# Up projection of a ConvFFN: two products of the next pair put between the third and fourth of the current one, and one weight sum moved from POOL to DVE

## The chip, the cores and the metric

The kernel runs on one core of a Trainium2 chip, in float32. The metric is the device time of one execution in microseconds; the time of a kernel is the median of its runs. TensorE is PE in the rows (its weight loads are PEld), VectorE is DVE, ScalarE is ACT, GpSimd is POOL and SyncE, which issues most DMAs, is SP.

## The reference, cut to what matters

One decoder block with three sublayers, each followed by a LayerNorm of `ALPHA * x + sublayer`: token mixing by two groups of heads, a cross-attention to a memory, and a gated ConvFFN. The change lies in the first half of the ConvFFN, on x of 1024 x 1024, `w_up` of 1024 x 5632 and a causal convolution of width 3:

```python
D_MODEL, SEQ, D_FF, CONV_WIDTH = 1024, 1024, 2816, 3

def _conv_ffn(x, w_up, conv_w, conv_b, w_down):
    u = jnp.einsum('bsd,df->bsf', x, w_up)
    ch = u.shape[-1]
    u = lax.conv_general_dilated(u, conv_w.reshape(CONV_WIDTH, 1, ch).astype(u.dtype),
                                 window_strides=(1,), padding=[(CONV_WIDTH - 1, 0)],
                                 dimension_numbers=('NWC', 'WIO', 'NWC'),
                                 feature_group_count=ch) + conv_b
    a, g = jnp.split(u, 2, axis=-1)
    return jnp.einsum('bsf,fd->bsd', jax.nn.silu(g) * a, w_down)
```

## The kernel before, in words

The stages follow one another: input projection, the two mixers, their output projection and LayerNorm, the cross-attention, its output projection and LayerNorm, then the up projection (with convolution and gate) and the down projection. Nothing is scheduled by hand between engines: the program is written in one order, a scheduler lays out each engine's queue from it, and an engine works its queue strictly in that order, waiting where an operand is not there. In the profiled execution the up projection lies at about 929 to 1383 us of the span.

**Pairs and products.** The up projection goes over NF = 22 pairs f of 128 columns of the a half and 128 columns of the g half of `w_up`. One pair is a 2x2 block product in the Strassen-Winograd form: seven block products in place of eight, on sums and differences of the blocks. On the weight side these are A11, A12, A22 (blocks as they are) and S3, S1, S2, S4 (sums and differences; S2 is made from S1, S4 from S2). On the side of x they are B11, B21, B22 and T3, T1, T2, T4, made once for all pairs. Each operand is split into a high part (a cast to fp32r) and a low part (the rest), and a product is 12 matmuls of 128x512 with 12 weight loads: for each of four k, high by high, high by low, low by high. The product's line is L1080.

**The order of a pair.** `begin(f)` does A11 with B11 into a bank of tag `S`, copies it to `ya` (L1089, ACT), does A12 with B21 into a bank of tag `pj` and adds it to `ya` (L1091, DVE). `end(f)` does S3 with T3 into a first `t` bank (copied to `yg` by L1109, ACT), S1 with T1 into a second `t` bank (added to `yg` by L1111, DVE), S2 with T2 on top of A11's bank (copied to `u` by L1114, ACT, and added to `yg` by L1115, DVE), A22 with T4 on top of S3's bank (L1117, DVE), and S4 with B22 on top of S1's bank (L1121, DVE). So A22 may not start before L1109 has read its bank, nor S4 before L1111 has. There are two `pj`, three `t` and three `S` banks. Between A22 and S4 the g half goes through its convolution (`conv`: L1099 on ACT, L1100 and L1101 on DVE) and silu (L1119, ACT); after S4 the a half goes through the convolution, L1123 multiplies the two, and L1125 writes `hid`. Up to pair 10 (HC = 11), L1128 also takes a difference for the down projection and L1129 writes it to `sum`. Before, the pairs stand as `begin(0)`, `begin(1)`, `end(0)`, `begin(2)`, `end(1)`, `begin(3)` and so on (LEAD = 2).

**The weights.** `Weights` makes them up to six (WAHEAD) ahead of their use, in the order of the products. For each product `load` takes the source, casts it to the high part on ACT (L1046) and subtracts on POOL to get the low part (L1047). A source is raw columns of `w_up` (a DMA, L1013, into one of three `raw` buffers) or a sum at L1024: S3 and S1 on POOL, S2 and S4 on DVE. The sums S1 and S2 share one slot (`sw`), S3 and S4 another.

**Slots.** Nearly every tile (`wop`, `sw`, `ya`, `yg`, `z`, `s3`, the operands) is one of 47 slots of equal size. They go round first in, first out, so a new tile waits for the last reader or writer of an old one in the same slot, also for a DMA that writes an old `z` or `s3` to memory.

**The operands of x.** B11 and B21 are made during the LayerNorm before. T3, T1, T2, T4 and B22 are made by `turn` at their first use, in pair 0: transposes on TensorE (L991), a copy on ACT (L993), a subtraction on DVE (L994).

The down projection follows in L1244, with operands made by L183 (ACT) and L185 (POOL or DVE). Its first weights go into slots that come free near the end of the up projection.

## Time and profile before

| | |
|---|---|
| runs | 1615.91, 1626.25, 1627.2 us; median 1626.25 us |
| profiled execution | 1620.13 us, of which its span is 1618.4 us |
| mean granted clock of TensorE | 0.988 of full speed |
| PE | 1552.2 us busy, 96% of the span |
| PEld | 1307.9 us, 81% |
| DVE | 1104.0 us, 68% |
| ACT | 739.8 us, 46% |
| POOL | 642.8 us, 40% |
| up projection, 929 to 1383 us: PE, DVE, POOL, ACT | 437.24, 330.54, 316.94 and 212.27 of 454.00 us |

The profile is one execution of its own, recorded by the hardware, so its time differs a little from the median; the execution's time is its span and 1.7 us around it. Busy shares are averages over stages with different limits. The matmuls of PE overlap one another, so PE counts as busy also where a short wait lies between two of them; the weight loads (PEld) show the waits more sharply.

### The profile page before, as it was taken

To read this page: it belongs to the slowest core of one execution; us is meant where nothing else is said; L and a number is where in the kernel's file an instruction comes from. 1 tells how busy PE (TensorE), PEld (TensorE's weight loads), DVE (VectorE), ACT (ScalarE), POOL (GpSimd) and SP (SyncE) were. 2 spreads that over 40 slices of the span, in tenths; PEclk is the share of its full clock that TensorE was granted. 3 is DMA by queue.
4 is the path that set the end of the run, shared out by engine and by line. 5 is a ranking of instruction groups with operands and counts; after the bars stand their busy time and mean duration, and the time that the engine had idled before them with its cause. 6 is when DMAs were issued, how large, how long until landed. Compare 5 with 4: busy or idle time off the path is not lost.

```text
span 1618.4 us, 21414 instructions
## 1 busy us (share of the span) xinstructions
PE 1552.2 (96%) x7949; PEld 1307.9 (81%) x7949; DVE 1104.0 (68%) x1734; ACT 739.8 (46%) x1317; POOL 642.8 (40%) x496
## 2 busy tenths in 40 slices
PE   8999999999998989999999999999989999999996
PEld 6788888888887988888978878777768888788884
DVE  4856967466667756642556567777777667987896
ACT  4725564255566751133542144444445455445531
POOL 5303222134435741111102657877778775000043
PEclk9999999999999999999999999999999999999998
DMA  5301112132141592311382222322223224875753
GB/s 183 79 1 27 53 53 59 47 92 67 52 118 46 170 267 89 120 40 52 104 263 92 78 66 69 100 86 87 89 94 95 79 79 134 282 245 184 235 189 104
DMA packets 166041, 176.67 MB, mean 109 GB/s; under 512 B 7761, under 2 KB 122521, under 8 KB 165937
## 3 DMA queue, kind: packets, MB, share of 16 engines
q1 hardware_dynamic: 162448, 163.61, 32.5%
q10 hardware_dynamic: 3168, 11.54, 1.9%
q8 instruction: 62, 1.02, 0.3%
q14 instruction: 43, 0.34, 0.1%
q0 software_dynamic: 320, 0.16, 0.1%
HBM read 132.77 MB, written 38.31 MB: 106 GB/s over the span
## 4 chain that ended last, share of the span: by engine, by line
PE 61%; DVE 15%; DMA 8%; POOL 6%; ACT 4%; issue 4%; SPq 1%; POOLq 0%; DVEq 0%; ACTq 0%
PE ps_pj L174 22%; PE ps_S L174 17%; PE ps_t L1080 7%; PE ps_t L174 5%; PE ps_S L1080 3%; POOL wop L1047 3%; DVE dop L185 2%; DMA raw<-hid 2%; POOL sw L1024 2%; DMA raw<-sumS 2%; DVE sw L1024 2%; PE ps_pj L1080 2%; PE ps_S L1244 1%; DVE z L1101 1%; DVE z L1100 1%
## 5 line engine op out<-in xcount | busy, mean ns | idle before, releaser
L174 PE MATMUL ps_pj<-xT,wh 128*128 128x512 f32 x976 | 313.6, 397 | 0.9 <-DVE KL L593 0.9
L174 PEld LDWEIGHTS ps_pj<-xT,wh 128*128 128x128 f32 x976 | 180.5, 189 | 35.2 <-DVE KL L593 1.4
L185 POOL TENSOR_TENSOR wl<-raw,wh 128x1024 fp32r<-128x1024 f32 x48 | 118.0, 2457 | 219.7 <-ACT wh L183 206.2
L174 PE MATMUL ps_pj<-xT,wl 128*128 128x512 f32 x488 | 193.0, 395 | 0.0
L1080 PE MATMUL ps_t<-T,wop 128*128 128x512 f32 x792 | 190.2, 391 | 1.5 <-ACT yg L1109 0.9
L1080 PEld LDWEIGHTS ps_t<-T,wop 128*128 128x128 f32 x792 | 148.1, 188 | 33.5 <-ACT yg L1109 1.3
L784 POOL TENSOR_SCALAR mv<-mv 128x1 f32<-128x1 f32 x24 | 27.0, 1123 | 342.0 <-DVE mv L783 342.0
L1047 POOL TENSOR_TENSOR wop<-raw,wop 128x512 fp32r<-128x512 f32 x66 | 119.7, 1826 | 94.4 <-ACT wop L1046 94.4
L1047 POOL TENSOR_TENSOR wop<-sw,wop 128x512 fp32r<-128x512 f32 x88 | 135.6, 1562 | 28.9 <-ACT wop L1046 28.9
L1244 PE MATMUL ps_S<-dop,dop 128*128 128x512 f32 x396 | 102.8, 405 | 8.8 <-DVE dop L185 6.0
L1046 ACT CAST wop<-sw 128x512 fp32r<-128x512 f32 x88 | 54.5, 621 | 124.1 <-POOL sw L1024 106.5
L174 PEld LDWEIGHTS ps_pj<-xT,wl 128*128 128x128 f32 x488 | 91.9, 188 | 17.7
L174 PE MATMUL ps_S<-wh,mh 128*128 128x512 f32 x256 | 100.1, 391 | 0.7 <-ACT mh L183 0.7
L174 PE MATMUL ps_S<-wh,ml 128*128 128x512 f32 x256 | 100.2, 392 | 0.0
L1244 PEld LDWEIGHTS ps_S<-dop,dop 128*128 128x128 f32 x396 | 76.8, 196 | 28.7 <-DVE dop L185 8.1
L174 PE MATMUL ps_S<-wl,mh 128*128 128x512 f32 x256 | 99.9, 390 | 0.0
L183 ACT CAST wh<-raw 128x1024 fp32r<-128x1024 f32 x64 | 67.2, 1049 | 61.2 <-issue 23.6
L1244 PE MATMUL ps_t<-dop,dop 128*128 128x512 f32 (+1 forms) x351 | 87.1, 378 | 1.7 <-DVE y L1295 1.7
L183 ACT CAST dop<-raw 128x512 fp32r<-128x512 f32 x77 | 47.7, 622 | 85.7 <-DVE raw L1209 44.9
L1080 PE MATMUL ps_t<-B,wop 128*128 128x512 f32 x264 | 68.9, 410 | 13.6 <-DVE yg L1111 13.6
L1244 PEld LDWEIGHTS ps_t<-dop,dop 128*128 128x128 f32 x351 | 63.5, 189 | 14.1 <-DVE y L1295 1.9
L1080 PEld LDWEIGHTS ps_t<-B,wop 128*128 128x128 f32 x264 | 50.8, 196 | 28.3 <-DVE yg L1111 17.8
(301 smaller groups left out, 3584.5 us busy)
## 6 DMA issues: line engine op xcount, KB each, us to landing
raw<-in_ffn_w_up_dram SPq DMA_DIRECT2D x44, 512.0 KB, 3.9
raw<-hid SPq DMA_DIRECT2D x66, 256.0 KB, 3.4
raw<-in_w_in_dram SPq DMA_DIRECT2D x24, 512.0 KB, 4.0
hid<-z SPq DMA_DIRECT2D x22, 512.0 KB, 2.6
wr<-in_ffn_w_down_dram SPq DMA_DIRECT2D x44, 256.0 KB, 4.7
raw<-sumS SPq DMA_DIRECT2D x44, 256.0 KB, 3.8
raw<-in_xa_wkv_dram SPq DMA_DIRECT2D x16, 512.0 KB, 4.4
x_dram<-y ACTq DMA_DIRECT2D x16, 512.0 KB, 2.6
```

The costliest lines, as they stand in the source:

```text
L174: nc.tensor.matmul(o, l, r, start=start, stop=stop)
L183: nc.scalar.copy(h, src)
L185: eng.tensor_tensor(l, src, h.bitcast(F32), ALU.subtract)
L784: nc.gpsimd.tensor_scalar(mv[:, 2:3], mv[:, 1:2], LN_EPS, None, ALU.add)
L1024: eng.tensor_tensor(sums[pair][:, i], x0, x1, op)
L1046: nc.scalar.copy(w[:, 0], src)
L1047: nc.gpsimd.tensor_tensor(w[:, 1], src, w[:, 0].bitcast(F32), ALU.subtract)
L1080: nc.tensor.matmul(ps, w[:, part, ws], r, start=first and k == 0 and i == 0, stop=k == 3 and i == 2, skip_group_check=not first)
L1100: nc.vector.scalar_tensor_tensor(z[:, 1:], y[:, :S - 1], c1, z[:, 1:], ALU.mult, ALU.add)
L1101: nc.vector.scalar_tensor_tensor(z[:, 2:], y[:, :S - 2], c0, z[:, 2:], ALU.mult, ALU.add)
L1244: nc.tensor.matmul(groups[g][t][:, lo:hi], x[:, xp, ss], w[:, wp, lo:hi], start=first and i == 0 and n == 0, stop=i == HC - 1 and n == 2, ...
```

## The change

Two things are changed. The first is the order of the products, and with it the order in which the weights are made: `begin(f + 1)` is called inside `end(f)`, after L1115 and ahead of A22, where `begin(f + 2)` stood behind `end(f)`. Before, the products of a pair and what followed were S3, S1, S2, A22, S4, then A11 and A12 of f + 2; now they are S3, S1, S2, then A11 and A12 of f + 1, then A22 and S4. `begin(0)` and `begin(1)` still stand ahead of the loop, so `end(0)` has no `begin` in it. B11 and B21 give back their slots after `end(20)`; before, it was after `begin(21)`. The second is that the sum S1 is made on DVE in place of POOL. `take` fills up its store of weights from the first `begin` on, by a list `begun` in place of `live`.

```diff
--- before.py
+++ after.py
@@ -1031,7 +1031,7 @@
             if name == "S3":
                 return add("S3", self.rawt(f, 0)[:, 0], self.rawt(f, 1)[:, 0], ALU.subtract, nc.gpsimd)
             if name == "S1":
-                return add("S1", self.rawt(f, 1)[:, 0], self.rawt(f, 1)[:, 1], ALU.add, nc.gpsimd)
+                return add("S1", self.rawt(f, 1)[:, 0], self.rawt(f, 1)[:, 1], ALU.add, nc.vector)
             if name == "S2":
                 return add("S2", sums["S1S2"][:, 0], self.rawt(f, 0)[:, 0], ALU.subtract, nc.vector)
             assert name == "S4"
@@ -1052,20 +1052,22 @@
             self.ready.append(((f, name), w))
 
         def take(self, f, name):
-            while self.todo and len(self.ready) < 1 + (self.ahead if live or name == "S3" else 0):
+            while self.todo and len(self.ready) < 1 + (self.ahead if begun else 0):
                 self.load()
             key, w = self.ready.pop(0)
             assert key == (f, name)
             return w
 
     LEAD = 2
-    first, later = [("A11", "B11"), ("A12", "B21")], [("S3", "T3"), ("S1", "T1"), ("S2", "T2"), ("A22", "T4"),
-                                                      ("S4", "B22")]
-    order = [(f, a) for f in range(LEAD) for a, _ in first]
+
+    first = ["A11", "A12"]
+    order = [(f, a) for f in range(LEAD) for a in first]
     for f in range(NF):
-        order += [(f, a) for a, _ in later]
-        if f + LEAD < NF:
-            order += [(f + LEAD, a) for a, _ in first]
+        order += [(f, a) for a in ("S3", "S1", "S2")]
+        if LEAD <= f + 1 < NF:
+            order += [(f + 1, a) for a in first]
+        order += [(f, a) for a in ("A22", "S4")]
+    begun = []
     weights = Weights(order, WAHEAD)
     live = {}
 
@@ -1090,6 +1092,7 @@
         product(f, "A12", "B21", pe, True)
         nc.vector.tensor_tensor(ya[:, hs(0)], ya[:, hs(0)], pe, ALU.add)
         live[f] = ya, yg, pa
+        begun.append(f)
 
     def conv(f, j, y):
 
@@ -1113,6 +1116,8 @@
         u = small.tile([P, 512], F32, tag="vT", name="u", bufs=1)
         nc.scalar.copy(u, pa)
         nc.vector.tensor_tensor(yg[:, hs(1)], yg[:, hs(1)], u, ALU.add)
+        if LEAD <= f + 1 < NF:
+            begin(f + 1)
         product(f, "A22", "T4", pc, False)
         nc.vector.tensor_tensor(yg[:, hs(0)], u, pc, ALU.add)
         zg = conv(f, 1, yg)
@@ -1154,11 +1159,9 @@
         begin(f)
     for f in range(NF):
         end(f)
-        if f + LEAD < NF:
-            begin(f + LEAD)
-            if f + LEAD == NF - 1:
-                for name in ("B11", "B21"):
-                    put(*[t for p in ops.pop(name) for t in p])
+        if f == NF - 2:
+            for name in ("B11", "B21"):
+                put(*[t for p in ops.pop(name) for t in p])
     for o in ops.values():
         put(*[t for p in o for t in p])
 
```

The changed file is a few lines longer. These lines of before read in it: L1080 as L1082, L1089 as L1091, L1091 as L1093, L1099 to L1101 as L1102 to L1104, L1109 as L1112, L1111 as L1114, L1114 as L1117, L1115 as L1118, L1117 as L1122, L1119 as L1124, L1121 as L1126, L1123 as L1128, L1125 as L1130, L1128 as L1133 and L1244 as L1247. L991, L1013, L1024, L1046 and L1047 keep their numbers. Note that L1091, L1117 and L1128 are other operations in the two files.

Three places show what it does to the queues. The first is DVE's queue around the convolutions of pair 4, whose g half is `z_9476` and whose a half is `z_9497`; `sw` are weight sums of a pair further on. Before:

```order
L1100 SCALAR_TENSOR_TENSOR z_9476<-yg_9219,cw,z_9476 128x1023
L1121 TENSOR_TENSOR ya_9218<-u,ps_t 128x512
L1101 SCALAR_TENSOR_TENSOR z_9476<-yg_9219,cw,z_9476 128x1022
L1100 SCALAR_TENSOR_TENSOR z_9497<-ya_9218,cw,z_9497 128x1023
L1101 SCALAR_TENSOR_TENSOR z_9497<-ya_9218,cw,z_9497 128x1022
L1091 TENSOR_TENSOR ya_9506<-ya_9506,ps_pj 128x512
L1123 TENSOR_TENSOR z_9497<-z_9497,z_9476 128x1024
L1128 TENSOR_TENSOR s_480_9503<-z_9497 128x512
L1111 TENSOR_TENSOR yg_9363<-yg_9363,ps_t 128x512
L1024 TENSOR_TENSOR sw_9583<-sw_9583,raw 128x512
L1024 TENSOR_TENSOR sw_9565<-raw,sw_9583 128x512
L1115 TENSOR_TENSOR yg_9363<-yg_9363,u 128x512
```

And in the changed kernel, from the same operation on `z_9476`:

```order
L1103 SCALAR_TENSOR_TENSOR z_9476<-yg_9278,cw,z_9476 128x1023
L1126 TENSOR_TENSOR ya_9277<-u,ps_t 128x512
L1104 SCALAR_TENSOR_TENSOR z_9476<-yg_9278,cw,z_9476 128x1022
L1024 TENSOR_TENSOR sw_9545<-raw 128x512
L1103 SCALAR_TENSOR_TENSOR z_9497<-ya_9277,cw,z_9497 128x1023
L1024 TENSOR_TENSOR sw_9545<-sw_9545,raw 128x512
L1104 SCALAR_TENSOR_TENSOR z_9497<-ya_9277,cw,z_9497 128x1022
L1114 TENSOR_TENSOR yg_9422<-yg_9422,ps_t 128x512
L1024 TENSOR_TENSOR sw_9527<-raw,sw_9545 128x512
L1128 TENSOR_TENSOR z_9497<-z_9497,z_9476 128x1024
L1118 TENSOR_TENSOR yg_9422<-yg_9422,u 128x512
L1133 TENSOR_TENSOR s_480_9503<-z_9497 128x512
```

Before, the two sums that DVE makes (S2, S4) stood together behind the whole pair and behind L1111 of the next one. Now there are three, S1, S2 and S4 in this order; S1 and S2 stand between the convolution's steps, and S4 behind L1114 (L1111 of before), which itself moved ahead of the multiplication.

The second place is ACT's queue between the silu of pair 4 and the first convolution step of pair 5 (`z_9620`), with the semaphores that each operation waits for. Those that begin with DMAHW count finished transfers. Before:

```order
L1119 ACTIVATE z_9476<-z_9476 128x1024 [waits DVE_49,Activation_49]
L1046 CAST wop_9529<-raw 128x512
L1046 CAST wop_9625<-raw 128x512 [waits DMAHW0_49]
L1109 COPY yg_9363<-ps_t 128x512 [waits PE_49]
L1046 CAST wop_9567<-sw_9565 128x512 [waits DVE_49,Pool_49]
L1046 CAST wop_9585<-sw_9583 128x512 [waits DMAHW1_49,Pool_49]
L1046 CAST wop_9604<-sw_9583 128x512 [waits DVE_49]
L1114 COPY u<-ps_S 128x512 [waits PE_49]
L1046 CAST wop_9655<-sw_9565 128x512 [waits DVE_49,PE_49]
L1099 ACTIVATE z_9620<-yg_9363,cb,cw 128x1024 [waits DMAHW6_49,DVE_49]
```

In the changed kernel, from the copy to `u` in pair 5:

```order
L1117 COPY u<-ps_S 128x512 [waits PE_49]
L1091 COPY ya_9565<-ps_S 128x512 [waits DVE_49,PE_49,Activation_49]
L1046 CAST wop_9653<-sw_9527 128x512 [waits DVE_49]
L1046 CAST wop_9588<-raw 128x512 [waits DMAHW3_49,DVE_49]
L1046 CAST wop_9570<-sw_9545 128x512 [waits DMAHW4_49]
L1046 CAST wop_9748<-raw 128x512 [waits DMAHW2_49,Pool_49]
L1046 CAST wop_9673<-sw_9671 128x512 [waits PE_49,Pool_49]
L1102 ACTIVATE z_9620<-yg_9422,cb,cw 128x1024 [waits DVE_49]
```

Before, one row stood between the copy to `u` (L1114) and L1099, a cast that waits for no transfer. Now six rows stand between the copy to `u` and L1102 (L1099 of before), five of them casts. Here `wop_9588` is a weight of A11, `wop_9570` one of S2; DMAHW3 and DMAHW4 in their waits are the writes of `hid` and `sum` from the pair before, whose slots these two weights take over.

The third place is TensorE's queue in pair 0, where the transposes (L991) of the first T operand end and those of the next begin; it is one piece of the difference:

```order
-L1080 MATMUL ps_pj<-B_347_8051,wop_8667 128x512 x2
-L1080 MATMUL ps_pj<-B_348_8052,wop_8667 128x512
-L1080 MATMUL ps_pj<-B_347_8051,wop_8667 128x512
-L1080 MATMUL ps_t<-T_395_8670,wop_8615 128x512
-L1080 MATMUL ps_t<-T_396_8671,wop_8615 128x512
+L1082 MATMUL ps_t<-T_398_8674,wop_8615 128x512
+L1082 MATMUL ps_t<-T_399_8675,wop_8615 128x512
 L991 MATMUL ps_t<-ident,t_361_8335 128x128
 L991 MATMUL ps_t<-ident,t_367_8411 128x128
 L991 MATMUL ps_t<-ident,t_377_8503 128x128
 L991 MATMUL ps_t<-ident,t_379_8571 128x128
```

The rows with `wop_8667` are the end of a whole product, A12 with B21 of pair 2, that stood between the transposes of T3 and the first product with it (`wop_8615`, S3 of pair 0). In the changed kernel it is gone from there, and S3 follows the transposes.

## Rows read from the trace of the kernel before

**Rows 1.** Table of waits, weight loads, 950 to 1380 us: us in total, times, longest.

```profile
PEld ps_t L1080 <- DVE yg L1111: 17.8, 10, 3.3
...
PEld ps_t L1080 <- ACT yg L1109: 1.3, 1, 1.3
```

**Rows 2.** Timeline of weight loads, products S4: start us, us, operation, [idle before <-releaser].

```profile
1025.61 4.18 PEld L1080 LDWEIGHTS ps_t<-B,wop 128*128 128x128 f32 x12 [3.30 <-DVE yg L1111]
...
1086.34 2.60 PEld L1080 LDWEIGHTS ps_t<-B,wop 128*128 128x128 f32 x12 [1.64 <-DVE yg L1111]
...
1106.88 2.62 PEld L1080 LDWEIGHTS ps_t<-B,wop 128*128 128x128 f32 x12 [1.62 <-DVE yg L1111]
...
1212.53 4.04 PEld L1080 LDWEIGHTS ps_t<-B,wop 128*128 128x128 f32 x12 [3.33 <-DVE yg L1111]
...
1252.13 2.68 PEld L1080 LDWEIGHTS ps_t<-B,wop 128*128 128x128 f32 x12
...
1271.17 2.68 PEld L1080 LDWEIGHTS ps_t<-B,wop 128*128 128x128 f32 x12
```

**Rows 3.** Busy time by engine around the first long gap; granted clock, DMA share, GB/s.

```profile
core 0: us, PE busy (x) PEld busy (x) DVE busy (x) ACT busy (x) POOL busy (x), PEclk, DMA share, GB/s
1022.35:1029.84 7.49, 4.61 (x14) 3.33 (x13) 4.54 (x5) 2.02 (x4) 5.31 (x4) 0.77 0.30 114
```

**Rows 4.** Chain of waits, 1075 to 1110 us: start us, us, what.

```profile
1080.98 4.15 POOL wop L1047 x2
1085.14 1.69 POOL sw L1024
...
1086.85 0.63 ACT wop L1046
...
1088.80 1.30 POOL sw L1024
...
1090.85 1.81 DVE sw L1024
...
1094.99 1.25 ACT z L1099
...
1097.55 0.60 DVE ya L1121
```

**Rows 5.** DVE's operations by line and shape, five pairs, 1086.34 to 1189.07 us.

```profile
line engine op names shapes xcount | busy us, mean ns | idle before us <-releasers
L1024 DVE TENSOR_TENSOR sw<-raw,sw 128x512 f32<-128x512 f32 x5 | 9.1, 1811 | 0.2
L1115 DVE TENSOR_TENSOR yg<-yg,u 128x512 f32<-128x512 f32 x5 | 8.9, 1778 | 0.0
...
L1128 DVE TENSOR_TENSOR s<-z 128x512 f32<-128x512 f32 x5 | 8.3, 1663 | 0.2
L1100 DVE SCALAR_TENSOR_TENSOR z<-yg,cw,z 128x1023 f32<-128x1023 f32 x5 | 6.4, 1284 | 6.6 <-ACT z L1099 6.6
...
L1024 DVE TENSOR_TENSOR sw<-sw,raw 128x512 f32<-128x512 f32 x5 | 3.5, 693 | 19.2 <-POOL sw L1024 19.2
...
L1111 DVE TENSOR_TENSOR yg<-yg,ps_t 128x512 f32<-128x512 f32 x5 | 3.4, 675 | 0.0
```

**Rows 6.** Timeline, POOL at 1090 us and DVE at 1378 us, columns as in group 2.

```profile
1090.82 4.69 POOL L1047 TENSOR_TENSOR wop<-sw,wop 128x512 fp32r<-128x512 f32 x3 [0.73 <-ACT wop L1046]
...
1378.53 1.22 DVE L1123 TENSOR_TENSOR z<-z,z 128x1024 f32<-128x1024 f32 x1
```

**Rows 7.** DMA issues of the whole span: KB each, median us from issue to landing.

```profile
raw<-in_ffn_w_up_dram SPq DMA_DIRECT2D x44, 512.0 KB, 3.9
...
hid<-z SPq DMA_DIRECT2D x22, 512.0 KB, 2.6
```

**Rows 8.** Timeline of pair 0, POOL and weight loads, around 940 us.

```profile
939.87 1.29 POOL L1024 TENSOR_TENSOR sw<-raw,raw 128x512 f32<-128x512 f32 x1 [6.45 <-DMA raw<-in_ffn_w_up_dram]
...
941.61 2.61 PEld L1080 LDWEIGHTS ps_pj<-B,wop 128*128 128x128 f32 x12
```

**Rows 9.** Timeline of PE where the down projection takes over.

```profile
1400.62 0.96 PE L1244 MATMUL ps_S<-dop,dop 128*128 128x512 f32 x3 [1.22 <-ACT dop L183]
...
1403.97 2.42 PE L1244 MATMUL ps_S<-dop,dop 128*128 128x512 f32 x6 [2.16 <-DVE dop L185]
```

## The prediction

> **What bounds the kernel now.** On the page TensorE is busy nearly all the time, so I looked for what it waits for in the up projection. The table of waits names one thing: the weight loads of L1080 waited ten times for L1111 on DVE, 17.8 us, and once for L1109 on ACT, 1.3 us [rows 1]. The timeline of the weight loads gives the shape. From pair 11 on the same product comes back after 19.04 us (1252.13 to 1271.17), which is seven products of 2.72 us each and no wait. In the pairs before, S4 with B22 is 1.6 us late, six pairs in a row like the two shown, and comes back after 20.54 us (1086.34 to 1106.88). Two gaps of 3.3 us are worse: the 12 loads behind them took 4.18 and 4.04 us where 2.68 is normal [rows 2]. Around the first one the granted clock averages 0.77, so part of that stretch ran at the lower of the two levels (1.2 instead of 2.4 GHz), and TensorE had idled just before [rows 3].
>
> Why is L1111 late? It reads the bank of S1's product, into which S4's product goes on adding, and it stands in DVE's queue behind work of the pair before. The chain of waits shows what holds that queue [rows 4]: two low parts on POOL (4.15), S3's sum there (1.69), a cast, S1's sum on POOL (1.30), and only then the last sum on DVE (1.81). S2's sum is where DVE stands still, 19.2 us in five pairs, 3.84 us in each [rows 5]. So up to pair 10 a ring through DVE, ACT and POOL sets the pair, and TensorE's wait is its shadow. Later pairs lack L1128, and the ring fits into TensorE's 19.04 us.
>
> **The change part by part.** Lines are those of the kernel before.
>
> *A, the products.* Between the end of S1 and the start of S4 there are now four products (10.88 us) where there were two (5.44). The largest lateness, 3.3 us [rows 2], lies inside the 5.44 us that are added, so if DVE comes no later than before, all these waits go: 17.8 + 1.3 = 19.1, plus 1.50 + 1.36 = 2.9 for the slow loads behind the two large gaps, less 0.04 at each of the 11 for normal spacing: **21.5 us**. Next in line is L1117, which reads the bank of S3 and A22. A pair takes two of the three `t` banks, so this one goes to S1 of the next pair, now 5.44 us behind the end of A22 where it was 10.88. An addition from such a bank takes 0.7 us [rows 5], so DVE may lag by some 4.6 us before TensorE feels it.
>
> *B, the sum.* POOL loses 22 sums of 1.30 us (1.69 when held up) [rows 4]. DVE gains 22 of the shape of S2's, which takes 0.69 us with POOL idle. The bound from above is 1.81, S4's sum beside a busy POOL [rows 5]. I take 0.69 and count POOL's turns in C. The 3.84 us of standing still go, since S1 and S2 now follow each other on one engine.
>
> *C, what DVE's ring costs now.* DVE and POOL take turns. S4's sum starts 0.03 us after a low part on POOL and takes 1.81 instead of 0.69, so it is held for 1.12 us, and POOL's three low parts there take 4.69 us instead of 3 x 1.30 [rows 4 to 6]. L1111, with one side in PSUM, is not held (0.675 on average) [rows 5]. Laid end to end, a pair's work on this common path was 9 x 1.30 = 11.7 us on POOL and, on DVE, 1.22 [rows 6] + 4 x 0.69 + 4 x 1.28 = 9.1: 20.8 in all. Now it is 8 x 1.30 + 9.8 = 20.2. From pair 11 on it was 20.1 before, and those pairs ran at 19.04, because neighbours overlap a little. So 20.2 can fit, barely. The Trainium skill, "SBUF — State Buffer", section "Who interferes with whom", puts this down to a pair of ports under an exclusive lock, which a DVE instruction with two SBUF inputs and a POOL instruction that reads SBUF contend for; the 1.81 and the 0.675 agree with it.
>
> The order of ACT shows a new ring. The casts of A11 and S2 now wait for the writes of `hid` and of `sum`, whose slots they reuse, and L1099 stands behind both. From the end of L1123: write 2.6 [rows 7], cast 0.6, A11's low part 1.30, S3's sum 1.30, cast 0.63, L1099 1.25, then on DVE 1.28 + 0.6 + 1.28 + 0.69 + 1.28 + 0.69 + 1.28 + 0.6 + 0.69 + 1.22 [rows 4 to 6]: 17.3 us, and 1.12 more for each of POOL's other six operations that DVE meets on the way. That makes 18.4 us with one, 19.5 with two, 20.6 with three, 21.7 with four. Before, three of DVE's operations were held for about a full turn (S4's sum, L1115, L1128) [rows 5], but the low parts of S2 and A12 now run during ACT's steps, so I take two. Nine pairs (2 to 10) at 19.5 lag by 0.5 x 9 = 4.1 us, which fits into the 4.6 us of A. DVE enters them late, though, as the gap of 3.3 us in pair 2 shows [rows 2]. So I count **2 us** back. Bounds: 0, and 9.4 (nine pairs at 20.6 lag by 14.0, less 4.6).
>
> *D, the first pair.* While DVE and ACT made the first T operand, TensorE had A12 of pair 2 to do (941.61, 2.61 us) [rows 8]. In the changed order S3 follows the transposes directly. The operand comes no sooner, so TensorE waits there: **2.7 us** back. Bounds: 0, if that product fills another gap of the first pair, and 5.4, if POOL, which now also does S3's sum of pair 1 ahead of S3's low part, adds as much again. POOL's wait for the weights there (6.45 us) [rows 8] stays.
>
> *E, the hand-over.* B11 and B21 give back their slots seven products ahead of the end instead of ten, which is 8.2 us later, and the first rows of the down weights go into slots that come free around then. TensorE already waits 1.22 and 2.16 us there [rows 9]. Most of the 8.2 us is covered by products still to come, and I add **1.5 us**, bounds 0 and 4.
>
> SP's queue keeps its order (hid, sum, two loads), and a load lands after 3.9 us [rows 7], about a pair ahead of its use. S1's sum now waits for that load on DVE, with L1100 and L1111 behind it; with that lead it costs nothing.
>
> Sum: 21.5 - 2.0 - 2.7 - 1.5 = 15.3 us. Against the profiled execution (span 1618.4 us, 1620.13 in all) that is 1604.8. That execution lies 6.1 us below the median of the three runs, 1626.25, so the forecast is **1611 us**.
>
> **The rivals.**
>
> 1. *TensorE bound throughout.* The ring stays below 19.04 us, A12 fills a gap of the first pair, the slots arrive in time: all 21.5 us come, 1604.8 on the scale of the median. For it: pairs from 11 on run like that with 20.1 us on the common path. Against it: they have neither L1128 nor the write of `sum`.
>
> 2. *DVE becomes the bound up to pair 10.* With three turns of POOL, 20.6 us a pair, 9.4 us come back instead of 2, and the time is 1618. TensorE's wait moves from L1111 to L1117. For it: three operations of DVE are held now. Against it: DVE no longer stands still for 3.84 us a pair.
>
> 3. *The turns decide, whoever adds.* The pair stays at 20.55 us and only the 4.6 us of slack are won: 9 x 1.51 - 4.6 = 9.0 come back, 1618, and 1621 with D at its bound. The Trainium skill, "Perfetto Trace Analysis", section "Optimizing Scalar/DVE Operations", says that moving work between GpSimd and DVE might not help, as they share a read port; by that rule this is the outcome. The trace bears it out for the turns, but not for the 3.84 us, which is a wait for a result.
>
> 4. *Slower, by the ring through the write of `hid`.* At four turns a pair (21.7 us) nine pairs lag by 23.9, less 4.6 is 19.3, and with D and E 23.5 us come back against 21.5: 1628. At five (22.8 us) it is 1638. The point from which it decides is 21.5 us a pair.
>
> **How the numbers follow.** Forecast 0.47 (its own range 1606 to 1615), rival 1 0.20, rival 2 0.20, rival 3 0.07, rival 4 0.06. Three runs of the kernel before span 11.3 us, so a median moves by some 5, and about 1% is what a measurement can tell from no change. The range of 1600 to 1624 takes in rivals 1 to 3 with that spread and leaves out rival 4 and the far ends. Faster by over 1% means below 1610: rival 1 and a good third of the forecast, 0.37. Slower by over 1% (above 1642.5) needs the far end of rival 4 or a mishap like it, 0.05. The rest is 0.58.
>
> **What would show it.** In the changed trace: no waits of TensorE for L1111; S2's sum on DVE at once behind S1's; pairs 2 to 10 at 19.0 to 19.6 us and later ones at 19.04; a gap of 2 to 4 us between the first transposes and S3's first product; no stretch with a granted clock below 0.9 between the first pair and the down projection. I am wrong if TensorE waits for L1117 by over 1 us a pair, if L1099 comes late behind casts that wait for the write of `hid`, or if pairs from 11 on take more than 19.1 us.

## The result and the profile after

The changed kernel is slower: 1630.66 us (median of 20 runs, 1626.33 to 1638.68) against 1618.49 us for the kernel before (20 runs, 1613.99 to 1630.04), a ratio of 1.0069 with a 95% interval of 1.0056 to 1.0083. The prediction said 1611, with a range of 1600 to 1624. The three runs that it was set against had a median 7.8 us above that of the 20, so what is to be explained is a step of +12.2 us where -15.3 was forecast. The profiled execution of the changed kernel has a span of 1626.2 us, against 1618.4.

The table of waits of the weight loads, 925 to 1410 us of the changed kernel, has the columns of [rows 1]:

```profile
PEld ps_S L1082 <- POOL wop L1047: 15.1, 9, 2.2
PEld ps_S L1247 <- ACT dop L183: 7.7, 1, 7.7
PEld ps_t L1082 <- DVE yg L1114: 6.1, 9, 0.7
PEld ps_t L1082 <- DVE T L994: 4.6, 2, 4.3
```

L1114 is L1111 of before. Its 17.8 us [rows 1] went down to 6.1, but 15.1 us of waiting for a low part on POOL took their place, 4.6 us came in the first pair and 7.7 at the hand-over to the down projection. The timeline of the weight loads gives the spacing, as in [rows 2]:

```profile
1088.18 2.63 PEld L1082 LDWEIGHTS ps_t<-B,wop 128*128 128x128 f32 x12 [0.71 <-DVE yg L1114]
...
1098.42 2.17 PEld L1082 LDWEIGHTS ps_S<-T,wop 128*128 128x128 f32 x10 [1.71 <-POOL wop L1047]
...
1109.44 2.63 PEld L1082 LDWEIGHTS ps_t<-B,wop 128*128 128x128 f32 x12 [0.68 <-DVE yg L1114]
...
1235.42 2.68 PEld L1082 LDWEIGHTS ps_t<-B,wop 128*128 128x128 f32 x12
...
1254.46 2.68 PEld L1082 LDWEIGHTS ps_t<-B,wop 128*128 128x128 f32 x12
```

S4 comes back after 21.26 us (1088.18 to 1109.44) where it was 20.54, and after 19.04 later on (1235.42 to 1254.46), as before. Two waits make the difference: S2's weight is 1.7 us late and S4 another 0.7.

To see where the time went, the way through the up projection is cut at the start of the first product and at S4 of pairs 4, 13 and 20 (counted back from the last S4, which is pair 21's; so counted, the rows of [rows 2] are pairs 3, 6, 7, 12, 14 and 15, and 19.04 us begins after pair 13, not 11 as the prediction has it):

| us | before | after | difference |
|---|---|---|---|
| first product to S4 of pair 4 | 116.87 | 120.07 | +3.20 |
| pair 4 to pair 13 | 186.92 | 189.90 | +2.98 |
| pair 13 to pair 20 | 133.28 | 133.28 | 0 |
| pair 20 to the end of the span | 252.03 | 257.50 | +5.47 |

The sum is 11.65 us. The changed kernel's profiled execution had reached its first product 3.85 us earlier (925.45 against 929.30 us), ahead of all that was changed, which leaves the 7.8 between the spans. Nine pairs at 19.04 are 171.36, so the middle stage still loses 18.5 us where it was to lose 2. All of it lies in pairs 5 to 12.

The profiled executions compared below reach their first product between 925.45 and 935.79 us, though no edit lies ahead of it, so the stages are compared beside the times.

The timeline shows one round of the ring, the closed chain of waits, that sets these pairs:

```profile
1088.76 0.38 SPq L1013 DMA_DIRECT2D raw<-in_ffn_w_up_dram  x1
1089.89 0.34 SPq L1130 DMA_DIRECT2D hid<-z  x1
...
1093.91 0.62 ACT L1046 CAST wop<-raw 128x512 fp32r<-128x512 f32 x1 [4.53 <-DMA hid<-z]
...
1094.61 1.30 POOL L1047 TENSOR_TENSOR wop<-raw,wop 128x512 fp32r<-128x512 f32 x1 [3.59 <-ACT wop L1046]
...
1095.86 1.29 POOL L1024 TENSOR_TENSOR sw<-raw 128x512 f32<-128x512 f32 x1
...
1097.10 1.27 POOL L1047 TENSOR_TENSOR wop<-sw,wop 128x512 fp32r<-128x512 f32 x1
...
1097.70 1.24 ACT L1102 ACTIVATE z<-yg,cb,cw 128x1024 f32<-128x1024 f32 x1
...
1099.04 1.66 DVE L1103 SCALAR_TENSOR_TENSOR z<-yg,cw,z 128x1023 f32<-128x1023 f32 x1 [5.68 <-ACT z L1102]
...
1108.71 0.67 DVE L1114 TENSOR_TENSOR yg<-yg,ps_t 128x512 f32<-128x512 f32 x1
...
1109.91 1.21 DVE L1128 TENSOR_TENSOR z<-z,z 128x1024 f32<-128x1024 f32 x1
...
1111.15 0.34 SPq L1130 DMA_DIRECT2D hid<-z  x1
```

From one write of `hid` to the next it is 21.26 us. ACT waits 4.53 us for the write to land, because A11's weight takes over the slot that is being written out. Behind that cast queue A11's low part and S3's sum on POOL, then S3's cast and L1102 on ACT, and DVE stands still for 5.68 us until L1102 is done. S2's low part (1097.10) is behind it on POOL, and TensorE's S2 starts when that part is there. The waits of ACT and DVE in 1050 to 1200 us say the same of seven pairs:

```profile
ACT wop L1046 <- DMA hid<-z: 33.4, 7, 5.0
```

```profile
DVE z L1103 <- ACT z L1102: 41.6, 7, 6.2
```

DVE stood still for 3.84 us a pair at S2's sum and 1.32 at L1100 [rows 5]; now the first is gone and the second is 5.9.

### The profile page after: what moved, and what is told of

It reads as the page before. It is cut to its first block, busy times and chain, and to the rows that moved or that the text cites. A ratio compares the mean times of both kernels' runs of the same rounds, so it can differ in the third digit from the quotient of the medians.

```text
span 1626.2 us, 21477 instructions
## 1 busy us (share of the span) xinstructions
PE 1550.8 (95%) x7949; PEld 1303.8 (80%) x7949; DVE 1130.3 (70%) x1756; ACT 735.7 (45%) x1317; POOL 589.4 (36%) x474
## 4 chain that ended last, share of the span: by engine, by line
PE 58%; DVE 19%; DMA 9%; issue 6%; ACT 5%; POOL 2%; SPq 0%; DVEq 0%; POOLq 0%; ACTq 0%
PE ps_pj L174 21%; PE ps_S L174 17%; PE ps_t L174 4%; PE ps_S L1247 3%; DMA hid<-z 3%; PE ps_S L1082 3%; DVE z L1103 3%; DVE dop L185 2%; DVE sw L1024 2%; PE ps_t L1247 2%; DVE z L1104 2%; PE ps_pj L1082 2%; DMA raw<-hid 2%; DVE z L1128 2%; PE ps_t L1082 1%
## 5 line engine op out<-in xcount | busy, mean ns | idle before, releaser
L1082 PE MATMUL ps_t<-T,wop 128*128 128x512 f32 x792 | 191.6, 392 | 9.1 <-DVE T L994 4.0
L185 POOL TENSOR_TENSOR wl<-raw,wh 128x1024 fp32r<-128x1024 f32 x48 | 118.0, 2459 | 217.5 <-ACT wh L183 207.6
L1082 PEld LDWEIGHTS ps_t<-T,wop 128*128 128x128 f32 x792 | 148.8, 189 | 41.7 <-DVE T L994 4.6
L1047 POOL TENSOR_TENSOR wop<-sw,wop 128x512 fp32r<-128x512 f32 x88 | 145.6, 1664 | 54.8 <-ACT wop L1046 54.2
L1047 POOL TENSOR_TENSOR wop<-raw,wop 128x512 fp32r<-128x512 f32 x66 | 93.6, 1425 | 133.7 <-ACT wop L1046 133.7
L1247 PE MATMUL ps_S<-dop,dop 128*128 128x512 f32 x396 | 104.0, 408 | 12.5 <-ACT dop L183 8.6
L1247 PEld LDWEIGHTS ps_S<-dop,dop 128*128 128x128 f32 x396 | 77.4, 197 | 32.5 <-ACT dop L183 10.2
L1247 PE MATMUL ps_t<-dop,dop 128*128 128x512 f32 (+1 forms) x351 | 87.6, 378 | 1.7 <-DVE y L1298 1.7
L1046 ACT CAST wop<-sw 128x512 fp32r<-128x512 f32 x88 | 53.2, 618 | 57.9 <-DVE z L1128 25.4
L1082 PE MATMUL ps_S<-T,wop 128*128 128x512 f32 x264 | 67.3, 395 | 11.4 <-POOL wop L1047 11.4
L1103 DVE SCALAR_TENSOR_TENSOR z<-yg,cw,z 128x1023 f32<-128x1023 f32 x22 | 40.9, 1859 | 49.4 <-ACT z L1102 49.4
L1247 PEld LDWEIGHTS ps_t<-dop,dop 128*128 128x128 f32 x351 | 63.6, 189 | 14.2 <-DVE y L1298 1.9
```

What stands on the lines that cost most here:

```text
L185: eng.tensor_tensor(l, src, h.bitcast(F32), ALU.subtract)
L1046: nc.scalar.copy(w[:, 0], src)
L1047: nc.gpsimd.tensor_tensor(w[:, 1], src, w[:, 0].bitcast(F32), ALU.subtract)
L1082: nc.tensor.matmul(ps, w[:, part, ws], r, start=first and k == 0 and i == 0, stop=k == 3 and i == 2, skip_group_check=not first)
L1103: nc.vector.scalar_tensor_tensor(z[:, 1:], y[:, :S - 1], c1, z[:, 1:], ALU.mult, ALU.add)
L1247: nc.tensor.matmul(groups[g][t][:, lo:hi], x[:, xp, ss], w[:, wp, lo:hi], start=first and i == 0 and n == 0, stop=i == HC - 1 and n == 2, ...
```

## The experiments

Three kernels (e2, e8, e11) have the old order of products; the others are the changed kernel with an edit. The last three columns are stages of the table above, read from the same view of each; pair 13 to pair 20 is 133.28 us in all of them. A ratio is estimated from all runs of a kernel against those of the kernel before made beside it (10 to 25 runs, medians of 1618.0 to 1620.3 us), so it is not the quotient of two medians of the table.

| kernel | median us | ratio to before (95%) | to pair 4 | 4 to 13 | 20 to end |
|---|---|---|---|---|---|
| before | 1618.49 | 1 | 116.87 | 186.92 | 252.03 |
| after | 1630.66 | 1.0069 (1.0056 to 1.0083) | 120.07 | 189.90 | 257.50 |
| e1 order alone | 1628.86 | 1.0068 (1.0036 to 1.0100) | 117.38 | 186.41 | 259.94 |
| e2 sum alone | 1614.29 | 0.9966 (0.9934 to 0.9998) | 115.01 | 181.06 | 251.96 |
| e3 both slots | 1612.97 | 0.9983 (0.9959 to 1.0006) | 123.02 | 172.26 | 255.50 |
| e9 slot of hid | 1619.37 | 0.9998 (0.9975 to 1.0022) | 119.59 | 177.11 | 258.10 |
| e10 slot of sum | 1622.74 | 1.0017 (0.9995 to 1.0039) | 122.76 | 182.60 | 255.19 |
| e4 early give-back | 1632.46 | 1.0081 (1.0052 to 1.0110) | 121.13 | 191.04 | 250.87 |
| e5 begin(2) early | 1629.10 | 1.0056 (1.0022 to 1.0089) | 118.58 | 188.82 | 257.60 |
| e6 first sums on POOL | 1626.69 | 1.0037 (1.0018 to 1.0056) | 118.20 | 191.00 | 257.78 |
| e12 both slots, give-back | 1606.88 | 0.9939 (0.9918 to 0.9960) | 122.83 | 173.26 | 249.94 |
| e7 all four repairs | 1604.77 | 0.9913 (0.9887 to 0.9938) | 118.31 | 173.80 | 250.78 |
| e8 sum, other slots | 1639.11 | 1.0114 (1.0084 to 1.0144) | 122.79 | 201.66 | 254.60 |
| e11 sum, late slots | 1616.97 | 0.9983 (0.9960 to 1.0006) | 121.88 | 182.38 | 249.54 |

**The two halves of the change.** e1 has the new order of products, with S1's sum on POOL:

```diff
-                return add("S1", self.rawt(f, 1)[:, 0], self.rawt(f, 1)[:, 1], ALU.add, nc.vector)
+                return add("S1", self.rawt(f, 1)[:, 0], self.rawt(f, 1)[:, 1], ALU.add, nc.gpsimd)
```

> The new order of products alone; S1's sum stays on POOL. Theory (three losses: a ring from the multiplication through the write of hid, the cast and low part of A11, S3's sum and S2's low part up to pair 12; the first pair; the hand-over): the ring loses one operation on DVE (0.69) and gains one on POOL (1.30), so pairs 5 to 12 take 21.3 to 22 us, the first T operand's low part is late by 2 to 3 us less, since one or two sums fewer stand ahead of it on DVE, the hand-over stays late: 1626 to 1633 us against 1618.5 before. Rival (the move of the sum to DVE causes the loss, by more operations of DVE held by POOL): pairs at or below 20.5 us and a time at or below 1619.

e2 is the kernel before with the sum alone on DVE (the opposite edit).

> S1's sum on DVE alone; the old order of products. Theory: the order of products makes the loss, and the sum by itself takes POOL's 1.30 us and a hand-over between engines out of the old ring, so the pairs that took 20.55 us come to 19.04 to 19.6, the first pair loses 2 to 3 us: 1603 to 1610 us. Rival (the turns of DVE and POOL set the pair, whoever adds): pairs stay at 20.3 to 20.6 us, TensorE waits for L1111 as before, 1618 to 1621.

e1's time came out inside the theory's range and its pairs 5 to 11 at 20.9 to 21.3 us, at the lower edge of what was expected or below it; the first pairs lose 2.7 us less than in the changed kernel. Its middle stage takes no more than before (186.41 and 186.92 us), so its loss is almost all at the hand-over, 7.9 us. It showed a wait there that the changed kernel has only in small (0.36 us). The timelines of weight loads and of DVE in e1:

```profile
1374.70 1.36 PEld L1082 LDWEIGHTS ps_t<-T,wop 128*128 128x128 f32 x4 [5.44 <-issue]
```

```profile
1373.30 0.69 DVE L185 TENSOR_TENSOR dop<-raw,dop 128x512 fp32r<-128x512 f32 x1 [0.91 <-ACT dop L183]
1373.91 0.68 DVE L1122 TENSOR_TENSOR yg<-u,ps_t 128x512 f32<-128x512 f32 x1
```

S1 of pair 21 starts right behind the end of L1122 (L1117 of before), whose bank it takes over. DVE had operands of the down projection (L185) in front of it.

e2 is faster than before (0.9966, an interval that barely leaves out 1; 7.8 us in the stages), but it missed both the time and the pair that were expected: its pairs take 19.92 us, with a wait of 1.0 for L1111 in each. The sum alone is a small gain, the new order alone a loss, and the two do not add up: in the old order the sum on DVE saves 5.9 us in the middle stage (186.92 to 181.06), in the new one it costs 3.5 (186.41 to 189.90) and 2.7 in the first pairs, against 2.4 saved at the hand-over. The chain of waits in e2 points at what holds the 19.92: S1's sum takes the slot of `s3` and waits for the write of `sum`.

```profile
1099.47 1.67 DVE s L1128
...
1101.16 2.01 DMA sumS<-s
...
1103.29 1.55 DVE sw L1024
```

**The ring through the writes.** e3 lets `begin` take the slots in another order, so that `ya` and `yg`, which are written late, get those of `s3` and of the product, and S2's and A11's weights those of the old `ya` and of the other `z`:

```diff
+        if LEAD < f <= HC + 1:
+            slots.free_list[:4] = [slots.free_list[i] for i in (2, 3, 0, 1)]
         ya, yg = get([P, S], name="ya"), get([P, S], name="yg")
```

> The changed kernel, but from pair 3 to pair 12 begin gives the slots of the old s3 and of the old product z (which wait for the writes of sum and hid) to ya and yg, and S2's and A11's weights take the slots that ya and yg had. Theory (the ring through the write of hid sets 21.4 us): the 4 us of the write leave the ring, pairs 5 to 12 take 19.04 to 19.4, and 15 to 19 us come back: 1611 to 1616 us. Rival (turns of DVE and POOL set the pair): pairs stay above 20.5 us, 1624 to 1631.

This is what happened: the pairs come to 19.04 us and the middle stage from 189.90 to 172.26, 0.9 above TensorE's own 171.36. Of the waits of the weight loads between 1045 and 1230 us one row is left in e3:

```profile
PEld ps_t L1082 <- ACT wop L1046: 1.0, 1, 1.0
```

No engine got an operation more or less by this edit, and DVE works its operations in the same order, so the turns of DVE and POOL don't set the pair. The other queues are laid out anew, though: on ACT the copy to `ya` (L1093, L1091 of the changed kernel) stands behind two casts that it stood ahead of, and on POOL S2's low part comes ahead of S3's sum. So e3 takes the wait out together with this order, and what each is worth is not separated. One wait for a write is left in e3, that of this copy, 2.7 us a pair, and the pair runs at 19.04 us with it (ACT, 1050 to 1200 us):

```profile
ACT ya L1093 <- DMA sumS<-s: 21.6, 8, 3.1
```

The swap also has a price ahead of pair 4, 123.02 us where the changed kernel has 120.07. In the way to S4 of pair 3 TensorE stands still once for 3.63 us, and the 12 loads behind take 4.77 us where 2.68 is normal; the granted clock is 0.85 from 1006.5 to 1030 us, where the changed kernel has 1.00. What that wait is for was not followed up.

```profile
1013.84 4.77 PEld L1082 LDWEIGHTS ps_t<-T,wop 128*128 128x128 f32 x12 [3.63 <-issue]
```

e9 moves only the slot of the product (the order is 0, 3, 2, 1), e10 only that of `s3` (2, 1, 0, 3):

> The changed kernel, with one of the two swaps of slots alone: A11's weight no longer takes the slot of the product that goes to hid (yg takes it); S2's weight keeps the slot of s3. Theory (of the two writes, that of hid is on the ring): pairs 5 to 12 at 19.04 to 19.8 us, 1611 to 1617. Rival (the write of sum, which lands last, is the one): pairs stay above 20.8.

> The other swap alone: S2's weight no longer takes the slot of s3 (ya takes it); A11's weight keeps that of the product. Theory: the ring through the write of hid stays, pairs at 21.0 to 21.6 us, 1627 to 1633. Rival (the write of sum): pairs at 19.04 to 19.8, 1611 to 1617.

e9's pairs 6 to 11 take 19.4 to 19.9 us, e10's pairs 7 to 11 take 20.4 to 20.6. The write of `hid` is the larger part, as expected: the middle stage comes down by 12.8 us in e9 and by 7.3 in e10. Both times missed their ranges, e9's by 2 us above, e10's by 4 below, and e10's pairs are 0.9 us shorter than the changed kernel's 21.4, though the cast still waits for `hid`. That doesn't show the write of `sum` to be on the ring of the changed kernel: in e10 the write of `hid` lands after 3.1 us instead of 4.2 (last section), which by itself is more than 0.9. e9 shows that the write of `sum` takes over once `hid` is out of the way (ACT, 1050 to 1200 us):

```profile
ACT wop L1046 <- DMA sumS<-s: 25.5, 8, 3.6
```

Both hold up casts in one queue, ACT's, and only when no cast waits for either does TensorE set the pair.

**The same from the other side.** e8 starts from e2 and gives S1's sum and weight two slots that came free earlier; by that, S2's weight falls on the slot of `s3`:

```diff
                 if pair not in sums:
+                    if pair == "S1S2" and LEAD <= f <= HC + 1:
+                        slots.free_list[:4] = [slots.free_list[i] for i in (2, 3, 0, 1)]
                     sums[pair] = get([P, 2, 512], name="sw")
```

> The old order of products, S1's sum on DVE, and the sum's tile and S1's weight take two slots that came free earlier in place of those of s3 and of the product. Theory (with the sum on DVE the pair of 19.92 us is a ring through the write of sum, on which S1's sum waits for its slot): 2 us leave the ring, the pairs come to 19.04 to 19.3, TensorE's waits for L1111 go, and 7 to 10 us come off 1614: 1604 to 1608. Rival (turns of DVE and POOL set 19.92): 1612 to 1616.

A miss, and the slowest of all. The timeline of ACT in e8 shows why (L1048 is the cast, L1101 the first step of the convolution):

```profile
1101.60 1.15 ACT L1048 CAST wop<-sw 128x512 fp32r<-128x512 f32 x2 [5.66 <-DMA sumS<-s]
1102.64 1.24 ACT L1101 ACTIVATE z<-yg,cb,cw 128x1024 f32<-128x1024 f32 x1
```

A cast at the head of ACT's queue waits 5.66 us for the write of `sum`, with L1101 behind it: a ring like that of the changed kernel, through the other write, in the old order. DVE's queue is laid out anew as well (S1's sum comes behind two additions that it preceded in e2), so the slots are not all that changed. e11 gives the slots of `s3` and of the product to the two `z` of the convolutions instead (order 2, 3, 4, 0, 5, 1):

> The old order of products with S1's sum on DVE, as in the one that was slower by its slots, but now the slots of s3 and of the product go to the tiles z of the convolutions, which are written ten microseconds after those writes, and no weight or sum takes them. Theory (a weight or a sum that takes a slot with a write in flight closes the ring, nothing else): pairs 4 to 13 at 19.04 to 19.4 us, no wait for L1111 over 0.3, 1600 to 1607 us. Rival (the turns of DVE and POOL set the pair in the old order): pairs at 19.9 or more, 1612 to 1618.

This was a miss as well. No cast waits for a write any more, but S1's sum stands at another place of DVE's queue here too, and DVE waits there for its load, which the chain of waits has on its way:

```profile
1096.13 0.75 DVE L1026 TENSOR_TENSOR sw<-raw 128x512 f32<-128x512 f32 x1 [3.91 <-DMA raw<-in_ffn_w_up_dram]
```

```profile
1090.54 5.49 DMA raw<-in_ffn_w_up_dram
```

Pairs 6 to 11 take 20.4 to 20.9 us, by a ring through a load. So the expectation that only the writes close a ring in the old order is wrong. e8 and e11 both take away the wait that e2's chain points at, and both close another ring, so no run confirms that it is what holds the 19.92.

**The hand-over.** e4 gives B11 and B21 back inside `end(20)`:

```diff
             begin(f + 1)
+        if f == NF - 2:
+            for name in ("B11", "B21"):
+                put(*[t for p in ops.pop(name) for t in p])
         product(f, "A22", "T4", pc, False)
```

> The changed kernel, but B11 and B21 give back their slots right behind begin(21), ahead of A22 and S4 of pair 20, so two products earlier. Theory (the hand-over loses some 5 us because the down projection's first rows get those slots late): 2 to 5 us come back, 1626 to 1629 us, and TensorE's wait of 7.7 us for a down weight shrinks below 4. Rival (the wait there comes from the order of DVE, ACT and SP at the end of the up projection, not from these slots): 1630 to 1631, the wait stays.

The time doesn't show it: at 1632.46 us it missed its range and can't be told from the changed kernel (1.0081, interval from 1.0052, against 1.0069). Its profiled execution came to the first product 9.6 us after the changed kernel's, with a lower granted clock between 200 and 300 us (0.92, where the changed kernel has 0.98), long before the edit; columns as in [rows 3]:

```profile
200.00:300.00 100.00, 95.10 (x541) 82.85 (x540) 70.74 (x91) 46.92 (x82) 24.48 (x17) 0.92 0.22 58
```

The stage does show it: from pair 20 to the end 250.87 us in place of 257.50, below the 252.03 of before. The wait of 7.7 us is gone from its place, and one of 4.1 for the same line comes later. In the changed kernel the windows behind the last S4 show a second price, TensorE's clock:

```profile
1384.24:1395.93 11.69, 4.40 (x19) 3.30 (x18) 10.81 (x17) 6.32 (x11) 0.00 (x0) 0.82 1.00 333
1395.93:1405.00 9.07, 8.71 (x26) 6.53 (x27) 9.07 (x14) 4.43 (x6) 0.00 (x0) 0.67 0.62 220
```

TensorE is busy 4.40 of 11.69 us there, and afterwards it works at a mean granted clock of 0.67, so largely at 1.2 GHz in place of 2.4. The kernel before has a smaller such stretch (0.88 from 1400.6 to 1415 us). e12 joins e3 and e4:

> The changed kernel with two of the four repairs: both slots swapped, and B11 and B21 given back early; the first pair stays as the change makes it. Theory (the ring and the hand-over are separate losses): pairs 4 to 11 at 19.04, the way from S4 of pair 20 to the end at 250 to 252 us as with all repairs, the first pair as late as in the changed kernel (S4 of pair 2 at 80 to 81 us): 1606 to 1610 us, some 3 us more than with all four. Rival (the early give-back wins nothing in a time, its own run did not come out lower): 1611 to 1614, as with the slots alone.

1606.88 us with 249.94 for the last stage: the repairs add up as expected, 6 us from e3's 1612.97 and 5.6 in the last stage.

**The first pairs.** In the changed kernel DVE's timeline has five weight sums ahead of the first T operand's low part:

```profile
936.02 0.69 DVE L1024 TENSOR_TENSOR sw<-raw 128x512 f32<-128x512 f32 x1 [1.87 <-DMA raw<-in_ffn_w_up_dram]
...
940.00 1.75 DVE L1024 TENSOR_TENSOR sw<-raw 128x512 f32<-128x512 f32 x1
...
943.35 0.68 DVE L994 TENSOR_TENSOR T<-ps_t,T 128x512 fp32r<-128x512 f32 x1
```

The two shown are S1's, of pairs 0 and 1. That low part starts 17.90 us behind the first product (925.45). In the kernel before it was 14.84 us (from 929.30):

```profile
944.14 0.68 DVE L994 TENSOR_TENSOR T<-ps_t,T 128x512 fp32r<-128x512 f32 x1
```

e6 leaves those on POOL (`nc.gpsimd if f < LEAD else nc.vector`); e5 puts `begin(2)` behind pair 0 and none into pair 1.

> The changed kernel, but S1's sums of pairs 0 and 1 are made on POOL. Theory (S1's sums of two pairs stand in DVE's queue ahead of the first T operand's low part): the wait of 4.3 us for L994 falls by some 2, as it did with all sums of S1 on POOL (2.3), and the way from the first product to S4 of pair 2 comes down from 80.7 to 78 to 79 us. Rival (DVE is held by POOL there, whoever adds): no change, 80 to 81.

> The changed kernel, but begin(2) stands behind the whole of pair 0 as before, and pair 1 has no begin in it; from pair 2 on the new order. Theory (the first pair loses 5.9 us, in part because A12 of pair 2 no longer fills the wait for the first T operand): the wait of 4.3 us for L994 falls below 2, and the way from the first product to S4 of pair 2 comes down from 80.7 by 2 to 4 us; pairs 5 to 12 stay at 21.4. Rival (the sums on DVE ahead of L994 alone make that loss): it stays above 80.

e6 does as expected: the wait for L994 falls from 4.3 to 2.3 us, and S4 of pair 2 comes 78.80 us behind the first product instead of 80.73. In e5 the wait falls to 0.7, but S4 of pair 2 comes no earlier (80.97): the filler is used in pair 0 and then missing later, as its weight loads show at pair 2 (there the product is L1084 and L1111 of before is L1116).

```profile
1013.51 0.30 PEld L1084 LDWEIGHTS ps_pj<-B,wop 128*128 128x128 f32 x2 [1.95 <-POOL wop L1047]
1015.79 4.77 PEld L1084 LDWEIGHTS ps_t<-B,wop 128*128 128x128 f32 x12 [1.98 <-DVE yg L1116]
```

So the filler moved the wait more than it removed it, and the range that was expected was missed. The low part itself starts 14.89 us behind the first product in e6 and 15.16 in e5, where three sums stand ahead of it; in e2, with S1's sums on DVE in the old order, it is 15.18. So it takes both halves of the change to make it late: the sums on DVE, and the order, which brings those of pair 1 forward. Up to S4 of pair 4, e5 still wins 1.5 of the 3.2 us, e6 1.9. What sets the first pairs was not settled further.

**All four repairs.**

> The changed kernel with four repairs: the slots of s3 and of the product go to ya and yg, B11 and B21 are given back early, begin(2) stands behind pair 0, S1's sums of pairs 0 and 1 are on POOL. Theory (three separate losses that add up): from the one with the slots alone (1613) another 4 to 5 us at the hand-over and 4 to 6 in the first pair: 1602 to 1606 us, pairs 4 to 20 at 19.04. Rival (the losses overlap, a later wait takes their place): 1609 to 1613.

1604.77 us, 0.9913 of the kernel before: the lowest time found, and faster than both kernels. Its pairs are not all at 19.04 us as expected; the middle stage is 173.80. With the repairs the new order comes out below the best time of the old one (e2's 1614.29), for which e8 and e11 found no repair. Against e12 the repairs of the first pairs bring 4.5 us up to pair 4 and lose 1.4 behind it; the medians lie 2.1 us apart, and their intervals overlap.

## Why the prediction was wrong

**What was right.** S2's sum no longer waits for POOL, though it doesn't follow S1's at once as said but a convolution step later; S1's sum costs 0.692 us on DVE (0.69 in B); pairs from 13 on stay at 19.04 us; the first two products of the next pair do cover L1111's lateness (17.8 us to 6.1). And the ring through the write of `hid` was found from ACT's order, with its members in the right sequence.

**The step that failed is the last one of C**, "So I count 2 us back". It added 17.3 us of work and two of POOL's turns to 19.5 us a pair. Measured is 21.26 in the pair shown and 21.47 on average of the five pairs below. Two terms were too small. The write was taken at 2.6 us [rows 7], a median over the old order; here it takes 4.0, with the second of SP's two loads, which were to cost nothing, issued 1.13 us ahead of it. And DVE is held for more: of its operations on the ring, five pairs (1066.74 to 1174.07 us) show these by line and shape, columns as in [rows 5]:

```profile
L1104 DVE SCALAR_TENSOR_TENSOR z<-ya,cw,z 128x1022 f32<-128x1022 f32 x5 | 11.5, 2305 | 0.0
L1024 DVE TENSOR_TENSOR sw<-sw,raw 128x512 f32<-128x512 f32 x5 | 8.9, 1785 | 0.0
...
L1104 DVE SCALAR_TENSOR_TENSOR z<-yg,cw,z 128x1022 f32<-128x1022 f32 x5 | 8.6, 1714 | 0.0
L1103 DVE SCALAR_TENSOR_TENSOR z<-yg,cw,z 128x1023 f32<-128x1023 f32 x5 | 8.3, 1657 | 29.5 <-ACT z L1102 29.5
```

Against 1.28, 0.69, 1.28 and 1.28 they are longer by 1.03, 1.10, 0.43 and 0.38, in all 2.9 us or 2.6 turns where two were taken. 17.3 + 1.4 + 2.9 is 21.6, of which small overlaps leave 21.3 to 21.5. Two microseconds a pair sound little, but at 19.5 the slack of 4.6 us swallows nine pairs, and at 21.3 it swallows two. Nor was that slack the right one: it was worked out for L1117, but TensorE felt the ring at S2's weight (15.1 us), a wait that the prediction doesn't name, and at L1111 (6.1). The upper bound (9.4 us, three turns) failed for the same reason: it bounded the turns and took the write as known.

The forecast for the middle stage was 15.6 us of gain less 2; it lost 3.0. That is 16.6 of the 27 us between forecast and result (-15.3 and +11.65 in the profiles).

**D, the first pair** was forecast at 2.7 us back, less the waits for L1111 that lie in the first four pairs, 0.79 in pair 2 and 3.30 with 1.5 of slow loads in pair 3. Measured are 3.2 us more instead of 2.8 less. The operand came no sooner, as written, but in fact 3.1 us later (17.90 for 14.84). "POOL, which now also does S3's sum" wasn't the cause: DVE's own sums were, brought forward by the new order; in e6, which undoes that, S4 of pair 2 comes 1.9 us earlier. B had moved 22 sums to DVE and looked at the pairs from 2 on alone. The wait that e6 leaves, 2.3 us, is near D's 2.7; why the way to pair 4 gained nothing from the waits for L1111 was not settled.

**E, the hand-over**, had the right mechanism but miscounted: seven products ahead of the end is where B21 is last read, while the program gives the slots back behind `end(20)`, five products ahead of the end, so later than E says in the round of slots. 1.5 us were forecast, at most 4, and 5.5 measured. e4 does put it seven products ahead; that takes back 6.6, and the way is then 1.2 us shorter than in the kernel before. So at E's own count nothing is lost.

**The rivals.** The fourth was the one that came: its mechanism, its 21.7 us a pair (measured 21.2 to 21.7 from pair 5 to 11), and 19.3 us back from the ring (18.5). It had 0.06, because it was tied to four turns; a longer write does the same with fewer. That its 1628 lies near the measured 1630.66 is in part luck: it stood 2 us above a median that was 7.8 too high, and the step of 12 has some 6 from D and 4 from E that it didn't have. Rival 3 falls by e3, where the pair is 19.04 with the same adders on the same engines. The Trainium skill, "Perfetto Trace Analysis", section "Optimizing Scalar/DVE Operations", warns that moving work between GpSimd and DVE might not help; here e2 shows a small gain, 20.55 to 19.92 us a pair, with DVE no longer standing still for POOL ahead of S2's sum.

The next in line that A named, L1117, was real and cost little in the changed kernel (0.36 us); e1 paid 5.44 for it.

## What to carry to other kernels

Where tiles share slots in turn, a new order of work also changes which new tile meets which old one: list for each slot who takes it over, and look first at those with a write to memory in flight, since the operation that waits for it holds up all that stands behind it in its queue. Price a transfer by what is issued next to it in the new order, not by its median in the old one. And when a ring is just below the bound, small errors in its parts decide the sign; bound every part of it, not only the one that seems uncertain.

## What the runs showed of the hardware

The same write of 512 KB takes 2.6 us by itself and 4.2, as a median, close behind a load. The lists of DMA issues, of the changed kernel in 1060 to 1180 us and in 1240 to 1360 us (columns as in [rows 7]):

```profile
raw<-in_ffn_w_up_dram SPq DMA_DIRECT2D x12, 512.0 KB, 3.9
hid<-z SPq DMA_DIRECT2D x6, 512.0 KB, 4.2
```

```profile
hid<-z SPq DMA_DIRECT2D x6, 512.0 KB, 2.6
```

In the first stretch a load of 512 KB is issued 1.13 us ahead of it (1088.76 and 1089.89 in the timeline of the ring), released by S4's sum, which stands just before the multiplication in DVE's queue; in the second the load is 3.3 us ahead. In e1 the load is 1.73 us ahead, and the write takes 3.5:

```profile
1085.78 0.38 SPq L1013 DMA_DIRECT2D raw<-in_ffn_w_up_dram  x1
1087.51 0.34 SPq L1130 DMA_DIRECT2D hid<-z  x1
```

In e10 it is 2.23 us ahead (1060 to 1180 us):

```profile
raw<-in_ffn_w_up_dram SPq DMA_DIRECT2D x12, 512.0 KB, 4.0
hid<-z SPq DMA_DIRECT2D x6, 512.0 KB, 3.1
```

In the kernel before no load is near it (the last one is issued 11.9 us ahead, the next 6.1 behind), and it is 2.6. Issue by issue, the write's landing follows the load's: in pairs 4 to 10 of the changed kernel, e1 and e10 it comes 1.25 to 1.30 us behind it, whichever of the three distances lies between the issues. The Trainium skill, "DMA: Bandwidth & Descriptors", section "Queues, rings and completion order", says that a DMA's semaphore increment lands only after every earlier write from the same DMA engine, across its queues; the rows agree with that. They fit a plain sharing of the engines less well, as the load hardly suffers: in these pairs it lands after 3.8 to 4.2 us beside the write and after 3.7 to 3.9 in the kernel before. The collision wasn't taken away by itself: no run moves the load and nothing else, so how much of the 21.26 us is due to it is only worked out (1.4).
